# Gate and up: weight sums by adding transfers with turned signs, and the first block product by quarter blocks

## The chip, the cores and the metric

The kernel runs on one core of a Trainium2 chip. A core has five engines that work side by side, each through its own list of instructions in order: TensorE (PE) multiplies, VectorE (DVE) adds and subtracts, ScalarE (ACT) copies and applies functions, GpSimd (POOL) and SyncE (SP) mostly start transfers. Engines wait for each other by semaphores. The metric is the device time of one execution in microseconds (us).

## The reference, cut to what matters

One encoder layer on 1024 tokens of width 1024, all in float32. An input projection feeds eight heads of bidirectional retention and eight of windowed attention, an output projection and a layer norm give h, and then comes the part that is changed:

```python
g = jnp.einsum('bsd,df->bsf', h, w_ffn_gate[i].astype(jnp.float32))
up = jnp.einsum('bsd,df->bsf', h, w_ffn_up[i].astype(jnp.float32))
ffn = jnp.einsum('bsf,fd->bsd', jax.nn.silu(g) * up, w_ffn_down[i].astype(jnp.float32))
```

The hidden width is 2816, that is 22 tiles of 128. An embedding branch is added, and a second layer norm closes the layer.

## The kernel before, in words

**Precision.** A float32 operand is split into a high half (ACT copies it, rounded to fp32r, L1338) and a low half (DVE subtracts the high half from the operand, L1351). A product is three matmuls: high by high, high by low, low by high (`mm3c`, L874 to L876). So each prepared weight costs one ACT and one DVE instruction, and the third matmul of a group is the first that reads the low half.

**Pairs and block products.** The 22 hidden tiles are taken as pairs 0 to 10. For a pair, and for gate (m = 0) and up (m = 1), the weights are a 2 x 2 of blocks (i, j), i the hidden tile and j the half of the width; h is a 2 x 2 of width half and token half. The four blocks of the result come from seven block products instead of eight (Strassen and Winograd's scheme), numbered 1 to 7. They need sums of weight blocks (products 5, 6, 7, 3) and sums of blocks of h, made once. A *unit* is one product for one m: 12 matmuls of 512 columns into one PSUM bank. Products 1, 6, 7 and 4 go one after the other into the same two banks (the chain, named `bmm` in the profile); 5 and 3 share two others (`bt`). After product 1, ACT copies the running sum out (s1, L1510), after 6 (u2, L1512), after 7 (u3, L1517).

**Quarter blocks.** Product 2 from pair 1 on, and product 4 from pair 2 on, use the scheme once more: gate and up are the two rows, and seven products of 256 columns go in four parts of 18, 6, 6 and 12 matmuls (`FINE`, `prep_fine`, `mm_fine`, `post_fine`). Their parts stand between whole units, so that DVE can add the banks (`bo` for product 2, `bs` for product 4) into the results between parts.

**Weights and sums.** SP loads block rows of 512 KB: (0, j) into tiles called `raw`, (1, j) into tiles called `ln`. `sums` makes four sums per m on DVE (L1373, L1374, L1376, L1377); the quarter blocks make three of 256 columns and a difference (L1396 to L1398, L1413).

**Order.** `plan` writes the order of the units by hand. Preparation (`Piece`) runs ahead of the units: after each unit, `ahead_g` issues pieces until the time that it reckons for the next unit is used up, as long as one of eight operand tiles (`oslots`) is free; a piece of the next unit is always issued. Within ACT and DVE the pieces and the work after the units (`post`, `urgent`) so form one list each, and an instruction that waits holds up all behind it. At a pair's end `sums_down` makes four sums of results for the down projection (L1480), stored by SP. POOL has nothing to do in this stage.

Of the kernel before, what the change touches and what calls it, by code (L numbers as in the profile page):

```python
# [47 lines left out]
def layer(tc, xT, xn, w_first, w_mt, w_rv, w_out, w_pg, w_pe, pT, w_gu, w_dn,  # L48
# [1222 lines left out]
    FROM = {2: 1, 4: 2}  # L1271
# [3 lines left out]
    homes, sums2 = {}, []  # L1275
# [12 lines left out]
    def fine_right(p, places):  # L1288
# [15 lines left out]
        def make(q, left, right):  # L1304
            def steps(x, c, us):
                def rows(pair):
# [6 lines left out]
                        piece(0, us, parts=lambda: [(x, *(v[:, c, :] for v in place(q)))])]  # L1313

            if p == 2 or q in (7, 5):
                return steps(fwide, slice(0, 2), 0.68)
# [8 lines left out]
    class Piece:  # L1325
# [5 lines left out]
        def issue(self):  # L1331
# [3 lines left out]
            if self.parts:  # L1335
                held.extend((self, x) for x in self.parts())
                for _, (x, hi, lo) in held:
                    act.activation(hi, x, AF.Copy)  # L1338
# [7 lines left out]
    def release():  # L1346
        for _, x in held:
            if callable(x):
                x()
            else:  # L1350
                dve.tensor_tensor(x[2], x[0], x[1].bitcast(F32), ALU.subtract)  # L1351
        held.clear()

    class Pair:


        def __init__(self, n):
            self.n = n
            self.raw, self.ops, self.bank, self.ev, self.s, self.fb = {}, {}, {}, {}, {}, {}
            self.fine = {2: {}, 4: {}}  # L1360

        def load(self, m, part=(0, 1)):
            for i in part:
                r = rawt(2 * HF) if i == 0 else ct([P, D], "ln", 2)
                sp.dma_start(r, w_gu[2 * self.n + i, m])
                for j in range(2):
                    self.raw[m, i, j] = r[:, j * HF:(j + 1) * HF]

        def sums(self, p, m):
            a = lambda i, j: self.raw[m, i, j]  # L1370
            s = self.s.setdefault(m, [sums2[m][:, 0, :], sums2[m][:, 1, :], a(1, 0), sums2[m][:, 0, :]])
            if p == 6:
                dve.tensor_tensor(s[1], a(1, 0), a(1, 1), ALU.add)  # L1373
                dve.tensor_tensor(s[0], s[1], a(0, 0), ALU.subtract)  # L1374
            else:
                dve.tensor_tensor(a(1, 0), a(0, 0), a(1, 0), ALU.subtract)  # L1376
                dve.tensor_tensor(s[0], a(0, 1), s[0], ALU.subtract)  # L1377

        def prep(self, p, m):
            a = lambda i, j: self.raw[m, i, j]  # L1380
            s = self.s.get(m)
            src = {1: lambda: a(0, 0), 2: lambda: a(0, 1), 4: lambda: a(1, 1), 5: lambda: s[1], 6: lambda: s[0],
                   7: lambda: s[2], 3: lambda: s[3]}[p]()
            t = self.ops[p, m] = take_op()
            return [(src, t[:, 0, :], t[:, 1, :])]

        def prep_fine(self, p, part):
# [3 lines left out]
            def xy():  # L1391
                return [self.raw[m, p == 4, 1] for m in range(2)]
# [677 lines left out]
```

## Time and profile before

| What | us |
|---|---|
| median of 3 runs (lowest, highest) | 1167.75 (1167.6, 1168.26) |
| profiled execution, its own time | 1168.96 |
| its span, first to last instruction | 1167.2 |
| first and last load of gate and up weights, start | 522.4, 896.7 |

The profile page has one line per group: line, engine, operation, output and inputs, count, then busy time and mean duration in ns, then idle time before it and what ended it. A time line has the start in us, the duration, the instruction, and in brackets the idle time before it and its releaser. Matmuls overlap: their recorded durations (about 390 ns for 512 columns) are longer than the distance of their starts, and it is the distance that counts. `bmm`, `bt`, `bo`, `bs` are PSUM banks, `w` and `u` operand tiles, `ev` results.

### The profile page before, as it was taken

What the parts mean: (1) busy time and instruction counts of PE and PEld (TensorE: products, weight loads), DVE (VectorE), ACT (ScalarE), POOL (GpSimd) and SP (SyncE); (2) the same over time, 40 slices, a digit from 0 to 9 for tenths busy, and PEclk for the clock granted to TensorE, in tenths of its full rate; (3) what the DMA queues carried; (4) which work ended last, traced back from release to release, by engine and by line L of the source; (5) the groups of instructions that cost most, each with busy time, mean ns of one, the idle gap of its engine ahead of it and who ended that gap; (6) DMA issues with size and microseconds to landing.
All of it is one profiled execution on the core that took longest, in us unless ns stands there. A gap on an engine that the chain in (4) does not pass through costs nothing.

```text
span 1167.2 us, 19086 instructions
## 1 busy us (share of the span) xinstructions
PE 1151.9 (99%) x6978; PEld 965.8 (83%) x6978; DVE 895.7 (77%) x1687; ACT 564.4 (48%) x1162; POOL 105.1 (9%) x118
## 2 busy tenths in 40 slices
PE   9999999999999999999999999999999999999997
PEld 7888878777888888888888888888888888888886
DVE  5556678594858898948999988888888876774778
ACT  5645367666546366214444433443344445552462
POOL 2000010102010021000000000000000011124242
PEclk9999999999999999999999999999999999999999
DMA  6346777666567955756322332332223289999978
GB/s 251 103 159 214 258 241 232 211 210 194 154 216 241 365 178 185 269 193 210 112 96 98 115 107 98 103 134 101 100 73 136 83 249 344 348 236 217 256 172 233
DMA packets 88863, 218.64 MB, mean 187 GB/s; under 512 B 12544, under 2 KB 20928, under 8 KB 88768
## 3 DMA queue, kind: packets, MB, share of 16 engines
q1 hardware_dynamic: 79984, 200.11, 49.6%
q0 software_dynamic: 8784, 17.31, 8.4%
q8 instruction: 55, 0.90, 0.3%
q14 instruction: 40, 0.33, 0.1%
HBM read 143.35 MB, written 62.19 MB: 176 GB/s over the span
## 4 chain that ended last, share of the span: by engine, by line
PE 89%; issue 4%; DMA 3%; DVE 2%; ACT 1%; SPq 1%; POOL 0%; DVEq 0%; POOLq 0%; ACTq 0%
PE bmm L875 8%; PE bmm L874 8%; PE bmm L876 8%; PE bt L874 6%; PE bt L875 6%; PE bt L876 6%; PE bmm L82 4%; PE bmm L84 4%; PE bmm L83 4%; PE bs L876 4%; PE bs L875 4%; PE bs L874 4%; PE bo L876 4%; PE bo L875 4%; PE bo L874 4%
## 5 line engine op out<-in xcount | busy, mean ns | idle before, releaser
L82 PE MATMUL bmm<-H,w 128*128 128x512 f32 x240 | 97.2, 405 | 0.1
L84 PE MATMUL bmm<-H,w 128*128 128x512 f32 x240 | 94.0, 392 | 0.5 <-issue 0.5
L83 PE MATMUL bmm<-H,w 128*128 128x512 f32 x240 | 94.0, 392 | 0.0
L1474 ACT ACTIVATE ev<-ev 128x512 f32<-128x512 f32 x42 | 26.5, 630 | 105.0 <-DVE ev L1503 91.8
L1648 POOL DMA_DIRECT2D h0b<-in_w_dn x24 | 21.6, 900 | 537.7 <-DVE ev L1454 503.6
L82 PEld LDWEIGHTS bmm<-H,w 128*128 128x128 f32 x240 | 45.2, 188 | 12.2 <-issue 1.9
L84 PEld LDWEIGHTS bmm<-H,w 128*128 128x128 f32 x240 | 45.0, 188 | 10.2
L83 PEld LDWEIGHTS bmm<-H,w 128*128 128x128 f32 x240 | 45.1, 188 | 7.8
L582 ACT ACTIVATE sc<-sc,st 128x384 f32<-128x384 f32 (+1 forms) x64 | 37.3, 586 | 17.1 <-DVE st L579 17.0
L579 DVE CUSTOM_DVE_ANT_0 sc<-cst,bs,nskb 128x384 f32<-128x384 f32 (+1 forms) x64 | 35.2, 575 | 7.0 <-PE bs L578 6.9
L1503 DVE TENSOR_TENSOR ev<-ev,bt 128x512 f32<-128x512 f32 x44 | 30.0, 682 | 12.5 <-PE bt L876 12.5
L622 ACT ACTIVATE ptr<-bt 128x384 f32<-128x384 f32 (+1 forms) x64 | 26.5, 456 | 25.5 <-PE bt L617 25.4
L1454 DVE TENSOR_TENSOR ev<-ev,bs 128x256 f32<-128x256 f32 x63 | 25.5, 416 | 15.6 <-PE bs L876 14.7
L1476 DVE TENSOR_TENSOR ev<-ev 128x512 f32<-128x512 f32 x42 | 29.0, 691 | 10.5 <-ACT ev L1474 9.0
L77 DVE TENSOR_TENSOR w<-raw,w 128x512 fp32r<-128x512 f32 x34 | 23.0, 687 | 17.3 <-ACT w L76 16.7
L874 PE MATMUL bmm<-H,u 128*128 128x512 f32 x92 | 36.1, 392 | 0.0
L875 PE MATMUL bmm<-H,u 128*128 128x512 f32 x92 | 36.0, 392 | 0.0
L876 PE MATMUL bmm<-H,u 128*128 128x512 f32 x92 | 35.8, 389 | 0.0
L874 PE MATMUL bmm<-H,w 128*128 128x512 f32 x84 | 32.9, 392 | 0.0
L875 PE MATMUL bmm<-H,w 128*128 128x512 f32 x84 | 32.9, 392 | 0.0
L876 PE MATMUL bmm<-H,w 128*128 128x512 f32 x84 | 32.7, 389 | 0.0
L1454 DVE TENSOR_TENSOR ev<-ev,bo 128x256 f32<-128x256 f32 x70 | 28.3, 416 | 5.2 <-PE bo L876 4.5
(832 smaller groups left out, 3836.8 us busy)
## 6 DMA issues: line engine op xcount, KB each, us to landing
ad<-ev SPq DMA_DIRECT2D x33, 512.0 KB, 2.6
pgd<-pro SPq DMA_DIRECT2D x28, 512.0 KB, 3.3
raw<-in_w_gu SPq DMA_DIRECT2D x22, 512.0 KB, 4.0
ln<-in_w_gu SPq DMA_DIRECT2D x22, 512.0 KB, 4.6
raw<-ad SPq DMA_DIRECT2D x40, 256.0 KB, 6.2
ln<-ad SPq DMA_DIRECT2D x37, 256.0 KB, 6.3
H<-in_w_dn SPq DMA_DIRECT2D x33, 256.0 KB, 9.2
wod<-aq SPq DMA_DIRECT2D x16, 512.0 KB, 2.7
```

The source lines that it names most:

```text
L82: pe.matmul(o, lh, rh, start=start, stop=False)
L83: pe.matmul(o, lh, rl, start=False, stop=False)
L84: recent[0] = pe.matmul(o, ll, rh, start=False, stop=stop).ins.name
L579: dve.tensor_tensor_reduce(sc[g][:, :nk], cst[:, tc0:tc0 + nk], b[:, :nk], slope(i, g), nskb[:, 2 * i + g:2 * i + g + 1], ALU.add, ALU.min ...
L582: act.activation(sc[g][:, :nk], sc[g][:, :nk], AF.Exp, bias=st_[:, 0, j, g:g + 1], scale=-1.0, accum_out=st_[:, 2, j, g:g + 1])
L622: act.activation(p_[:, :hi - lo, :], tb[:, :hi - lo, :], AF.Copy)
L874: pe.matmul(o, lh, rh, start=start, stop=False, skip_group_check=True)
L875: pe.matmul(o, lh, rl, start=False, stop=False, skip_group_check=True)
L876: pe.matmul(o, ll, rh, start=False, stop=stop, skip_group_check=True)
L1454: dve.tensor_tensor(out_, x, b, ALU.add)
L1476: dve.tensor_tensor(c[:, 1, :], c[:, 0, :], c[:, 1, :], ALU.mult)
L1503: dve.tensor_tensor(get(name), ev[left][:, m, :], right, ALU.add)
```

## The change

**Signs.** The first block row is taken with turned sign: with A' = (-A00, -A01; A10, A11) all four sums of the scheme become sums of plain blocks: A10 + A11, then + A00, then + A01, and A00 + A10, the last two used with a minus. So each can grow in place: a transfer on POOL's queue with `accum_op=ALU.add` (`grow`) adds a block from memory onto the block that lies in SBUF, as soon as its last reader has prepared it (`after`). The DVE sums are gone; there are 88 such transfers of 256 KB. The minus sits in ACT's copy (`scale=-1.0`) and in DVE's low half (`scalar_tensor_tensor`).

**Product 1 by quarter blocks** from pair 4 on (`FROM[1] = 4`). Its result is s1 in SBUF (`post_first`), and `seed` copies it with ACT, negated, into the two chain banks, into which product 6 then accumulates. The fine difference is written into the (0, 0) block, so SP loads that block again before it grows.

**Order.** Product 5 moves ahead of 6, 7 follows, and product 1 of the next pair is woven into the end of a pair. From pair 4 on a pair reads: (5,0), 1 part 2, 2 part 0, 1 part 3, (5,1), 2 part 1, (6,0), 2 part 2, (6,1), 2 part 3, (7,0), (7,1), 4 part 0, (3,0), 4 part 1, (3,1), 4 part 2, next 1 part 0, 4 part 3, next 1 part 1, with parts numbered from 0. Operand tiles go from eight to seven. The core of the diff:

```diff
-    FROM = {2: 1, 4: 2}
+    FROM = {2: 1, 4: 2, 1: 4}
...
-                    act.activation(hi, x, AF.Copy)
+                for _, (x, hi, lo, *sign) in held:
+                    act.activation(hi, x, AF.Copy, scale=-1.0 if sign else 1.0)
...
+            elif len(x) == 4:
+                dve.scalar_tensor_tensor(x[2], x[0], -1.0, x[1].bitcast(F32), ALU.mult, ALU.subtract)
...
-        def sums(self, p, m):
-            a = lambda i, j: self.raw[m, i, j]
-            s = self.s.setdefault(m, [sums2[m][:, 0, :], sums2[m][:, 1, :], a(1, 0), sums2[m][:, 0, :]])
-            if p == 6:
-                dve.tensor_tensor(s[1], a(1, 0), a(1, 1), ALU.add)
-                dve.tensor_tensor(s[0], s[1], a(0, 0), ALU.subtract)
-            else:
-                dve.tensor_tensor(a(1, 0), a(0, 0), a(1, 0), ALU.subtract)
-                dve.tensor_tensor(s[0], a(0, 1), s[0], ALU.subtract)
...
+        def load(self, m, i, js=(0, 1)):
+            if (m, i) not in raws:
+                raws[m, i] = rawt(2 * HF) if i == 0 else ct([P, D], "ln", 2)
+            c = slice(js[0] * HF, (js[-1] + 1) * HF)
+            sp.dma_start(raws[m, i][:, c], w_gu[2 * self.n + i, m][:, c])
...
+        def grow(self, m, to, by):
+            pool.dma_start(self.block(m, *to), self.weights(m, *by), accum_op=ALU.add)
...
+        def after(self, p, m):
+            if p == 1:
+                if self.n >= FROM[1]:
+                    self.load(m, 0, (0,))
+                self.grow(m, (0, 0), (1, 0))
+            elif p == 5:
+                self.grow(m, (1, 0), (0, 0))
+            elif p == 6:
+                self.grow(m, (1, 0), (0, 1))
+            elif self.n + 1 < NP:
+                following = pairs2[self.n + 1]
+                if p == 7 and m:
+                    for k in range(2):
+                        following.load(k, 0)
+                elif p == 3:
+                    following.load(m, 1, (0,))
+                    following.grow(m, (1, 0), (1, 1))
+                elif p == 4:
+                    following.load(m, 1, (1,))
...
-            return [[piece(0, 1.16, main=sums), piece(1, 0.62, parts=whole), piece(1, 0.36, parts=lambda: put(5, fsum[0]))],
-                    [piece(1, 0.36, parts=lambda: put(6, fsum[1]))],
+                for m in range(2):
+                    self.after(p, m)
+
+            return [[piece(1, 0.62, parts=whole), piece(0, 1.16, main=sums), piece(1, 0.36, parts=lambda: put(5, fsum[0]))],
+                    [piece(1, 0.36, parts=lambda: put(6, fsum[1])), piece(0, 0.36, main=difference)],
                     [piece(0, 0.36, parts=lambda: put(7, fsum[2], 6))],
-                    [piece(1, 1.1, main=difference, parts=last, then=loads)]][part]
+                    [piece(1, 0.74, parts=last, then=loads)]][part]
...
+        def post_first(self, part):
+            if part == 0:
+                self.begin()
+                self.ev["s1"] = self.h["s1"]
+            (c11, c12), (c21, c22) = ([self.ev["s1"][:, m, j * Q:(j + 1) * Q] for j in range(2)] for m in range(2))
+            (ba, bb), bz = [self.fb[1][0][:, j * Q:(j + 1) * Q] for j in range(2)], self.fb[1][1][:, :Q]
+            if part == 0:
+                act.activation(c11, ba, AF.Copy)
+                dve.tensor_tensor(c11, c11, bb, ALU.add)
+            elif part == 1:
+                act.activation(c12, ba, AF.Copy)
+            elif part == 2:
+                act.activation(c22, ba, AF.Copy)
+                dve.tensor_tensor(c22, c22, bz, ALU.add)
+            else:
+                dve.tensor_tensor(c12, c12, bz, ALU.add)
+                act.activation(c21, ba, AF.Copy)
...
+        def seed(self):
+            for m in range(2):
+                self.bank[0, m] = bank(TAGS[0])
+                act.activation(self.bank[0, m], self.ev["s1"][:, m, :], AF.Copy, scale=-1.0)
...
+                if m and self.n >= FROM[1]:
+                    self.seed()
...
+    def plan():
+        two = lambda n, p: [(n, p, 0), (n, p, 1)]
+        fine = lambda n, p, *parts: [(n, p, None, j) for j in parts]
+        def start(n):
+            return fine(n, 1, 0) + fine(n, 1, 1) if n >= FROM[1] else two(n, 1)
+        u = start(0)
+        for n in range(NP):
+            a, b, c = two(n, 5), two(n, 6), two(n, 7) + (two(n, 4) if n < FROM[4] else [])
+            f = fine(n, 2, 0, 1, 2, 3)
+            if n < FROM[2]:
+                u += two(n, 2) + a + b
+            elif n < FROM[1]:
+                u += [f[0], a[0], f[1], a[1], f[2], b[0], f[3], b[1]]
+            else:
+                h = fine(n, 1, 2, 3)
+                u += [a[0], h[0], f[0], h[1], a[1], f[1], b[0], f[2], b[1], f[3]]
+            u += c
+            e, s = two(n, 3), start(n + 1) if n + 1 < NP else [None, None]
+            if n < FROM[4]:
+                u += e + s
+            else:
+                f = fine(n, 4, 0, 1, 2, 3)
+                u += [f[0], e[0], f[1], e[1], f[2], s[0], f[3], s[1]]
+        return [x for x in u if x]
...
```

**What stands where now.** Three places on which the prediction rests, all at the turn from pair 6 to pair 7; the turns from pair 3 to 4 up to 9 to 10 read alike. Names: `ev` results, `bs` the banks of product 4 (901 to 922) or product 2, `bo903` and `bo904` product 1's banks, `raw799` and `raw810` block row 0 of gate and of up, `ln811` and `ln812` block row 1, `cst` and `fs` quarter sums, `w` and `u` operand tiles. In brackets stand the semaphores waited for: `DMAHW` for SP's transfers, `DMASW` for POOL's, each in turn over eight numbers.

DVE, before, from the additions after product 4's last part (two L1454) on:

```order
L1454 TENSOR_TENSOR ev837_5573<-ev837_5573,bs922_7640 128x256
L1454 TENSOR_TENSOR ev837_5573<-ev842_5578,bs921_7639 128x256
L1476 TENSOR_TENSOR ev837_5573<-ev837_5573 128x512
L1480 TENSOR_TENSOR ev837_5573<-ev837_5573,ev841_5577 128x512
L1480 TENSOR_TENSOR ev841_5577<-ev837_5573,ev838_5574 128x512
L1480 TENSOR_TENSOR ev838_5574<-ev838_5574,ev837_5573 128x512
L1503 TENSOR_TENSOR ev840_5576<-ev840_5576,bt924_7692 128x512
```

DVE, changed, from the same additions (two L1478) on:

```order
L1478 TENSOR_TENSOR ev837_5575<-ev837_5575,bs902_7822 128x256
L1478 TENSOR_TENSOR ev837_5575<-ev842_5580,bs901_7821 128x256
L1529 TENSOR_TENSOR ev837_5575<-ev837_5575 128x512
L1533 TENSOR_TENSOR ev837_5575<-ev837_5575,ev841_5579 128x512
L1533 TENSOR_TENSOR ev841_5579<-ev837_5575,ev838_5576 128x512
L1533 TENSOR_TENSOR ev838_5576<-ev838_5576,ev837_5575 128x512
L1533 TENSOR_TENSOR ev840_5578<-ev840_5578,ev841_5579 128x512
L1417 TENSOR_TENSOR cst_367<-raw810_5485 128x256
L1418 TENSOR_TENSOR cst_367<-cst_367,raw799_5418 128x256
L1419 TENSOR_TENSOR fs834_5572<-raw799_5418,raw810_5485 128x256
L1355 TENSOR_TENSOR w821_5559<-raw799_5418,w821_5559 128x512
```

The fourth sum of results moved up, and the three quarter sums of the next product 2 and the low half of its first operand (`w821`) stand right behind the sums; behind them come one addition (L1501) and three low halves of 256, the last two for product 1's last part (`u826`). Before, the next product 2's quarter sums (L1396 to L1398) and the low half of its first operand stood five to thirteen instructions ahead of these additions, and three whole units lay between product 4's last part and product 2.

ACT, before, around the copies after product 6 (L1512) and after product 1 (L1510), with the bank to be read named after the arrow:

```order
L1510 ACTIVATE ev840_5576<-bmm938_8114 128x512 [waits PE_49]
L1338 ACTIVATE u822_5558<-ln931_7954 128x512 [waits DMAHW7_49,DVE_49,Activation_49]
L1338 ACTIVATE w823_5559<-raw930_7858 128x256 [waits Activation_49]
L1338 ACTIVATE w823_5559<-cst_367 128x256 [waits DVE_49]
L1512 ACTIVATE ev842_5578<-bmm937_8089 128x512 [waits DMAHW2_49,PE_49]
```

ACT, changed, around the new copies into the banks of product 6 (L1510, bank before the arrow):

```order
L1340 ACTIVATE u822_5560<-fs834_5572 128x256 [waits DVE_49]
L1340 ACTIVATE w825_5563<-ln812_5490 128x512 [waits DMASW5_49,Activation_49]
L1340 ACTIVATE w821_5559<-raw810_5485 128x256 [waits DVE_49,Activation_49]
L1340 ACTIVATE w821_5559<-raw799_5418 128x256 [waits DVE_49]
L1510 ACTIVATE bmm909_8055<-ev839_5577 128x512 [waits DVE_49]
L1510 ACTIVATE bmm910_8057<-ev839_5577 128x512 [waits Activation_49]
```

The copy of product 1 now writes the banks, and ahead of it stand three high halves; the first of them (`w825`, for the second unit of product 6) waits for a transfer of POOL's (`DMASW5`), the third in the list below.

POOL, changed (before, its list is empty here):

```order
L1380 DMA raw799_5418<-in_w_gu 128x512 [waits DMAHW1_49,DMAHW7_49,DMASW3_49,DVE_49]
L1380 DMA raw810_5485<-in_w_gu 128x512 [waits DMAHW2_49,DMAHW0_49,DMASW4_49]
L1380 DMA ln812_5490<-in_w_gu 128x512 [waits DMASW1_49,DVE_49]
L1380 DMA ln811_5487<-in_w_gu 128x512 [waits DMASW6_49,DMASW2_49,DVE_49]
L1380 DMA ln812_5490<-in_w_gu 128x512 [waits DMASW7_49,DMASW5_49,DVE_49]
```

The first two wait for SP's reloads of `raw799` and `raw810` (`DMAHW1`, `DMAHW2`), which in turn wait on SP for DVE's low halves of `u826`; the third, `ln812`, is queued behind them.

More of the change, by code (lines that the diff above doesn't have):

```diff
@@ L1274, in layer @@
     TAGS = {0: "t", 1: "o", 2: "mm", 4: "s"}
-    homes, sums2 = {}, []
+    homes, raws = {}, {}
+    AT = {1: (0, 0), 2: (0, 1), 4: (1, 1)}
+    made = set()
     def next_homes():
@@ L1312, in steps @@
                         piece(0, us, main=lambda: subtract(1)),
-                        piece(0, us, parts=lambda: [(x, *(v[:, c, :] for v in place(q)))])]
-            if p == 2 or q in (7, 5):
+                        piece(0, us, parts=lambda: [(x, *(v[:, c, :] for v in place(q)))], then=lambda: made.add((p, q)))]
+            if p == 2 or p == 4 and q in (7, 5):
                 return steps(fwide, slice(0, 2), 0.68)
@@ L1358, in __init__ @@
             self.n = n
[L1359 to L1367, printed above, removed]
-        def sums(self, p, m):
-            a = lambda i, j: self.raw[m, i, j]
-            s = self.s.setdefault(m, [sums2[m][:, 0, :], sums2[m][:, 1, :], a(1, 0), sums2[m][:, 0, :]])
-            if p == 6:
-                dve.tensor_tensor(s[1], a(1, 0), a(1, 1), ALU.add)
-                dve.tensor_tensor(s[0], s[1], a(0, 0), ALU.subtract)
-            else:
-                dve.tensor_tensor(a(1, 0), a(0, 0), a(1, 0), ALU.subtract)
-                dve.tensor_tensor(s[0], a(0, 1), s[0], ALU.subtract)
+            self.ops, self.bank, self.ev, self.fb = {}, {}, {}, {}
@@ L1391, in xy @@
             def xy():
-                return [self.raw[m, p == 4, 1] for m in range(2)]
+                return [self.block(m, *AT[p]) for m in range(2)]
             def sums():
@@ L1540, in g_unit @@
         pr = pairs2[n]
-        def loads():
-            if n + 1 < NP and p == 7 and m:
-                for j in range(2):
-                    pairs2[n + 1].load(j, (0,))
-        def more():
-            if n + 1 < NP and p == 4:
-                pairs2[n + 1].load(m, (1,))
-        items = [piece(1, 0.62, parts=lambda: pr.prep(p, m), then=more)]
-        if p in (6, 7):
-            items.insert(0, piece(0, 1.42 if p == 6 else 1.24, main=lambda: pr.sums(p, m), behind=loads))
-        after = {2: (0.62, 1.4), 5: (0.62, 1.4), 4: (0, 2.8), 3: (0.62, 2.1)}.get(p, (0, 0))[m]
+        items = [piece(1, 0.62, parts=lambda: pr.prep(p, m), then=lambda: pr.after(p, m))]
+        after = {2: (0.62, 1.4), 7: (0.62, 1.4), 4: (0, 2.8), 3: (0.62, 2.1)}.get(p, (0, 0))[m]
         return items, lambda: pr.mm(p, m), lambda: pr.post(p, m, k), 2.72, after
@@ L1943, in layer @@
         fine, more = fine_right(2, halves4[:3]), fine_right(4, halves4[3:])
-        fine += more
+        fine += more + fine_right(1, [(t[:, 0], t[:, 1]) for t in halves1])
         homes.update((name, a_tile([P, 2, HF], "ev")) for name in ("spare", "s1", "u2", "c11", "u3", "c22"))
-        FINE4 = len(plan(0)) + len(plan(1)) - 2
-        FINES = (2, 4, 7, 9, 20, 23, 26, FINE4)
+        fours = units.index((FROM[4] - 1, 4, 1))
+        FINES = (2, 4, 7, 9, 16, 19, 22, fours, fours + 3, fours + 8, fours + 13, units.index((FROM[1] - 1, 1, 1)))
         ahead_g(-1, 4)
```

91 lines of the change are left out of this document (47 added, 44 removed).

## The prediction

> **What bounds the kernel now.** I read the page's busy times first, then the gate-and-up stretch (about 530 to 930 us) by windows, then single instructions of that stretch in order of time.
>
> ```profile
> PE 1151.9 (99%) x6978; PEld 965.8 (83%) x6978; DVE 895.7 (77%) x1687; ACT 564.4 (48%) x1162; POOL 105.1 (9%) x118
> ```
> ```profile
> 600.00:700.00 100.00, 100.00 (x532) 86.40 (x531) 89.30 (x179) 41.84 (x85) 0.00 (x0) 1.00 0.28 99
> 700.00:800.00 100.00, 100.00 (x548) 87.09 (x547) 83.42 (x173) 42.61 (x87) 0.00 (x0) 1.00 0.29 99
> 800.00:900.00 100.00, 100.00 (x548) 87.09 (x547) 85.36 (x174) 44.02 (x90) 0.00 (x0) 1.00 0.35 119
> ```
>
> In the windows the columns are PE, PEld, DVE, ACT, POOL, then granted clock, DMA share and GB/s. PE has no gap. DVE is at 83 to 89 of 100 us, POOL is empty, DMA is below 0.35. So only two things change the time here: less PE work, or an operand that comes after PE wants it. DVE has 11 to 17 us of slack in 100, so its order decides whether an operand is late.
>
> **The change, part by part.** *PE, removed.* From pair 4 on, seven times, product 1 goes from two whole units to quarter blocks.
>
> ```profile
> 705.20 0.28 PE L874 MATMUL bo<-h0b,w 128*128 128x256 f32 x1
> ...
> 706.63 0.40 PE L874 MATMUL bmm<-H,w 128*128 128x512 f32 x1
> ...
> 709.38 0.28 PE L874 MATMUL bs<-h,u 128*128 128x256 f32 x1
> ...
> 711.53 0.40 PE L874 MATMUL bt<-H,w 128*128 128x512 f32 x1
> ```
> ```profile
> 762.82 0.39 PE L874 MATMUL bmm<-h0a,w 128*128 128x512 f32 x1
> ...
> 765.53 0.39 PE L874 MATMUL bmm<-h0a,u 128*128 128x512 f32 x1
> ...
> 768.25 0.28 PE L874 MATMUL bo<-h0b,w 128*128 128x256 f32 x1
> ```
>
> These are the first matmuls of units, so their distances are unit lengths. A whole unit (12 matmuls of 512) takes 2.71 us, two take 5.43. A quarter part of 18 matmuls takes 2.15, one of 12 takes 1.43, so one of 6 takes 0.72: together 2.15 + 2 x 0.72 + 1.43 = 5.02. Gain 0.41 a pair, 7 x 0.41 = **2.9 us**. That is all PE can give.
>
> *DVE, removed.* The four weight sums per product side go:
>
> ```profile
> L1374 DVE TENSOR_TENSOR sums<-sums,raw 128x512 f32<-128x512 f32 x22 | 15.2, 692 | 0.8
> L1373 DVE TENSOR_TENSOR sums<-ln 128x512 f32<-128x512 f32 x22 | 15.0, 684 | 0.0
> L1377 DVE TENSOR_TENSOR sums<-raw,sums 128x512 f32<-128x512 f32 x22 | 15.0, 683 | 0.0
> L1376 DVE TENSOR_TENSOR ln<-raw,ln 128x512 f32<-128x512 f32 x22 | 15.0, 683 | 0.0
> ```
>
> 60.2 us over eleven pairs, 5.5 a pair. Behind a full PE this is worth nothing by itself. It covers the right-hand quarter sums of product 1 (32 adds of 256 on DVE, 13 us at 0.42 each, made during pairs 0 to 3, where 22 us went); without that cover they would cost up to those 13 us. The sign (STT instead of TT) is free if it is priced like the row
>
> ```profile
> L959 DVE SCALAR_TENSOR_TENSOR acc<-acc,h0b 128x512 f32<-128x512 f32 x12 | 7.6, 684 | 0.0
> ```
>
> *First wait, DVE at the turn of a pair.* PE's new order after the last part of product 4 is: product 1 part 1 (0.72), first unit of product 5 (2.72), product 1 part 2 (0.72), then product 2 part 0.  Set t = 0 at the end of product 4's last part. PE reaches product 2 at 4.16, and its third matmul, which reads the low half, at 4.16 + 2 x 0.12 = 4.40. On DVE the order printed above puts ahead of that low half: two adds, the multiply after Silu, four sums, three quarter sums.
>
> ```profile
> 744.07 0.40 PE L874 MATMUL bmm<-H,u 128*128 128x512 f32 x1
> ```
> ```profile
> 744.27 0.75 DVE L1454 TENSOR_TENSOR ev<-ev,bo 128x256 f32<-128x256 f32 x2 [0.49 <-PE bo L876]
> ...
> 752.97 0.42 DVE L1396 TENSOR_TENSOR cst<-raw 128x256 f32<-128x256 f32 x1
> 753.42 0.42 DVE L1397 TENSOR_TENSOR cst<-cst,raw 128x256 f32<-128x256 f32 x1
> 753.76 0.42 DVE L1398 TENSOR_TENSOR fs<-raw,raw 128x256 f32<-128x256 f32 x1
> 754.10 0.68 DVE L1351 TENSOR_TENSOR u<-raw,u 128x512 fp32r<-128x512 f32 x1
> ...
> 762.24 0.69 DVE L1476 TENSOR_TENSOR ev<-ev 128x512 f32<-128x512 f32 x1 [1.08 <-ACT ev L1474]
> 762.97 2.02 DVE L1480 TENSOR_TENSOR ev<-ev,ev 128x512 f32<-128x512 f32 x3
> ```
> ```profile
> 744.72 0.63 ACT L1474 ACTIVATE ev<-ev 128x512 f32<-128x512 f32 x1 [0.77 <-DVE ev L1454]
> ```
>
> The adds start 0.20 after PE goes on (744.27 - 744.07). Silu starts 0.45 later and takes 0.63: 1.28. Multiply to first sum 0.73: 2.01. Three sums 2.02, the fourth 0.67: 4.70. Three quarter sums 1.13 (752.97 to 754.10): 5.83. Low half 0.68: **6.5**. PE waits 6.5 - 4.4 = **2.1 us**, every one of the seven times. Before, those quarter sums and that low half ran ahead of product 4's last additions, with three whole units (2.71 each) to spare.
>
> *Second wait, the transfers.* Behind that low half DVE does one add and three low halves of 256 (0.34 apart), so product 1's last operand is ready at 7.9. Only then may SP reload the (0,0) blocks, since the fine difference was written into them. POOL's queue then holds three adding transfers in this order: two onto the reloaded blocks, which must wait for the reloads, and behind them the one that product 6, second unit, needs.
>
> ```profile
> raw<-in_w_gu SPq DMA_DIRECT2D x22, 512.0 KB, 4.0
> ...
> ad<-ev SPq DMA_DIRECT2D x11, 256.0 KB, 2.0
> ...
> raw<-in_w_rv SPq DMA_DIRECT2D x8, 256.0 KB, 2.6
> ```
> ```profile
> L1648 POOL DMA_DIRECT2D h0b<-in_w_dn x24: 866/875/1194, 945.9 to 1120.6; - x24
> ...
> DMA to landing us min/median/max: 4.2/7.0/8.6
> ```
> ```profile
> q0 software_dynamic: 1440, 2.62, 24.6%
> ```
>
> The reload is 256 KB: between 2.6 (the 256 KB load) and 4.0 (the 512 KB one); I take 3.3, so it lands at 11.2, its twin 0.3 later. POOL issues take 0.88 each: 11.3, 12.2, third at 13.1. An adding transfer lands 4.2 to 7.0 after its issue, in the down stage, where SP's loads run beside it. Ten of them took 24.6% of 60 us of 16 engines (the last row, window 940 to 1000), 1.48 each, so the third may wait up to 2 x (1.48 - 0.88) = 1.2 for the two ahead. DMA is quiet here, so I take the minimum and half the queue: 13.1 + 4.2 + 0.6 = **17.9** (bounds 16.6, with the reload at 2.6 and no queue, and 20.8, with 4.0 and 7.0). [...]
>
> Who waits: ACT. Its next instruction is the high half of product 6's second unit, from that transfer. Behind it stand two copies of 256 and then the new copy of product 1 into the banks of product 6, and the *first* unit of product 6 cannot start without that copy.
>
> ```profile
> 777.61 0.62 ACT L1338 ACTIVATE w<-sums 128x512 fp32r<-128x512 f32 x1
> 778.14 0.41 ACT L1338 ACTIVATE u<-cst 128x256 fp32r<-128x256 f32 x1
> 778.44 0.62 ACT L1338 ACTIVATE w<-sums 128x512 fp32r<-128x512 f32 x1
> ```
>
> From landing to the copied bank: 0.53 + 0.30 + 0.30 + 0.62 = 1.75. PE starts product 6 at 19.7 (18.4 to 22.6). Without any wait it would be there at 4.16 + 2.15 + 1.43 + 2.72 + 0.72 = 11.2. Both waits together cost 19.7 - 11.2 = **8.5 us a turn** (7.2 to 11.4), 2.1 of it at product 2 and 6.4 in one piece at product 6. Nothing later gets it back: PE is the bound for the rest of the pair, and the next turn starts from PE's own end of product 4.
>
> *The clock after 6.4 us of idle.*
>
> ```profile
> 1.31 3.60 PE L147 MATMUL bo<-sq 128*128 128x512 bf16 x8 [1.31 <-POOL sq L144]
> 4.91 0.63 PE L82 MATMUL bmm<-H,w 128*128 128x512 f32 x1
> 5.37 0.39 PE L82 MATMUL bs<-H,w 128*128 128x512 f32 x1
> ```
> ```profile
> 236.45 0.44 PE L577 MATMUL bs<-k,aq 128*128 128x384 f32 x1 [1.68 <-DVE pt L446]
> ```
>
> At the kernel's start nine 512-column matmuls took 5.37 - 1.31 = 4.06 us, 0.45 each, twice the later 0.226 (2.71/12), although the clock column says 1.00. Such a restart loses 4.06 - 9 x 0.226 = 2.0 us. After the longest idle inside the kernel, 1.68 us, there is none. An idle of 6.4 is nearly four times that, nearer to a start than to a pause, so I take the 2.0 and keep 0 as the other end. [...]
>
> *At nothing.* 88 POOL issues (77 us) fall into an empty POOL. The new ACT work lies in ACT's slack (busy 42 to 44 of 100). In pairs 1 to 3 the same transfer follows product 5 without a reload: 7 us from issue, against three units and more until product 6's second half; at most 1 us in all.
>
> **The sum.** 7 x (8.5 + 2.0) - 2.9 = 70.6 us. The profiled execution of before took 1168.96 (span 1167.2), 1.2 above the median of 1167.75. From the median: **1238 us**.
>
> **Rivals.**
> (a) Both waits, no slow restart: 7 x 8.5 - 2.9 = 56.6, 1224 us. For it: the clock column reads 1.00 everywhere. Against it: the start. [...]
> (b) Transfers as slow as in the down stage (landing at 20.8): 7 x (11.4 + 2.0) - 2.9 = 91, 1259 us. For it: the median of 7.0. Against it: a DMA share of 0.3 here.
> (c) Only DVE is late, the transfers arrive in time: 7 x 2.1 - 2.9 = 11.8, 1180 us. It needs the third landing before about 11.6 (13.4, when PE gets there, less 1.75), 1.5 us before I have even its issue; only a much faster reload path would do it.
> (d) The other side, faster: 1167.75 - 2.9 = 1165. It decides if the three quarter sums and the low half of product 2 run on DVE ahead of the pair's last sums and the reload starts at t = 0 or earlier. The trace shows PE without any gap under a fuller DVE, which speaks for slack; the printed order of DVE and POOL speaks against it.
>
> **How the numbers follow.** Forecast 0.50, (a) 0.16, (b) 0.16, (c) 0.12, (d) 0.04, and 0.02 for a balance near zero. About 0.2% (2.3 us) is what a measurement of this kernel can tell from no change; (d) is just past it. Faster 0.04, same 0.02, slower 0.94. The forecast alone spans 7 x (7.2 + 0) - 2.9 = +47 to 7 x (11.4 + 2.0) - 2.9 = +91; I stretch this to 1195 and 1265, which leaves out (c), (d) and zero: 0.18.
>
> **What would show it.** In the changed profile: seven PE idles before product 6's first unit (first matmul of the bank chain), each about 6 us and released by ACT's copy; seven of about 2 us before product 2's third matmul, released by DVE's low half; ACT idle before a high half "from ln", released by a DMA; 512-column matmuls at 0.45 just after the long idles. In windows, PE below 85 in 100 from the fourth pair on and full before it. I am wrong if PE is full at the turn of pair 3 to 4, if the adding transfers land within 2 us, or if the idles stand elsewhere than at these two places.

## The result, and the profile after

The changed kernel takes 1252.86 us (median of 6 runs, 1251.13 to 1257.86) against 1167.78 for the kernel before in the same comparison (6 runs, 1167.54 to 1168.45): 1.0735 times as long, 95% interval 1.0715 to 1.0755, that is 85 us slower. Forecast were 1238, with 1195 to 1265 as the range. The profiled execution has a span of 1250.9 us, 83.7 more than before (1167.2).

The page's busy times first, then the waits of PE in the gate-and-up stretch (engine and line that waits, engine and line it waits for, then us in total, times, longest):

```profile
PE 1177.1 (94%) x7104; PEld 991.0 (79%) x7104; DVE 882.8 (71%) x1708; ACT 582.8 (47%) x1226; POOL 182.5 (15%) x206
```
```profile
PE bmm L874 <- ACT bmm L1510: 42.8, 7, 6.9
PE bs L876 <- DVE w L1355: 13.1, 7, 1.9
PE bs L874 <- DVE ev L1478: 3.4, 2, 3.1
PE bmm L874 <- ACT ev L1574: 2.0, 1, 2.0
```

PE had 99% and no gap; now it waits seven times for ACT's copy into product 6's banks (L1510) and seven times for DVE's low half (L1355), once each in every turn from pair 3 to 4 on. The last two rows are in no turn: two waits at pair 10's end (L1478), and one in pair 0 (L1574). These totals, and the brackets of the time lines, count idle time from the end that the profile gives the matmul before. From here on a wait is counted by distances of starts instead, beyond the distance of a full rate; that gives about 0.16 us more for each, 2.03 us where the bracket says 1.88.

By windows (columns as in the prediction):

```profile
540.00:690.00 150.00, 148.05 (x754) 126.22 (x753) 123.80 (x252) 67.89 (x135) 28.01 (x32) 1.00 0.66 157
690.00:740.00 50.00, 41.19 (x236) 36.32 (x236) 31.76 (x69) 18.93 (x42) 7.08 (x8) 0.93 0.56 137
740.00:790.00 50.00, 42.09 (x233) 37.27 (x232) 32.06 (x70) 18.94 (x42) 7.07 (x8) 0.90 0.53 132
```

Up to the fourth pair PE is full but for 2 us; then 8 to 9 of 50 us are lost, and the granted clock, 1.00 all through this stretch before, falls to 0.90 to 0.93. One turn in order of time, that from pair 4 to 5, with t = 0 at 739.86, the end of product 4's last part and the start of the next product 1's part 1. PE at t = 0, then DVE and SP:

```profile
739.86 0.28 PE L874 MATMUL bo<-u,u 128*128 128x256 f32 x1
```

```profile
741.91 2.62 DVE L1533 TENSOR_TENSOR ev<-ev,ev 128x512 f32<-128x512 f32 x4
744.45 0.42 DVE L1417 TENSOR_TENSOR cst<-raw 128x256 f32<-128x256 f32 x1
...
745.58 0.69 DVE L1355 TENSOR_TENSOR w<-raw,w 128x512 fp32r<-128x512 f32 x1
...
746.85 0.75 DVE L1355 TENSOR_TENSOR u<-raw,u 128x256 fp32r<-128x256 f32 x2
```
```profile
747.63 15.99 SPq L1373 DMA_DIRECT2D raw<-in_w_gu  x4
```

POOL, ACT and PE, with the third of POOL's transfers (issued at 753.01) in the view of DMA issues (KB each, us from issue to landing):

```profile
751.78 1.77 POOL L1380 DMA_DIRECT2D raw<-in_w_gu  x2 [15.60 <-DMA raw<-in_w_gu]
753.01 1.45 POOL L1380 DMA_DIRECT2D ln<-in_w_gu  x1
```
```profile
ln<-in_w_gu POOLq DMA_DIRECT2D x1, 256.0 KB, 6.0
```
```profile
759.14 0.63 ACT L1340 ACTIVATE u<-ln 128x512 fp32r<-128x512 f32 x1 [7.22 <-DMA ln<-in_w_gu]
...
760.28 1.10 ACT L1510 ACTIVATE bmm<-ev 128x512 f32<-128x512 f32 x2
```
```profile
746.32 0.39 PE L876 MATMUL bs<-h0b,w 128*128 128x256 f32 x1 [1.88 <-DVE w L1355]
...
747.13 0.34 PE L876 MATMUL bs<-H,u 128*128 128x256 f32 x1
747.27 0.42 PE L874 MATMUL bs<-H,u 128*128 128x256 f32 x1
747.48 0.42 PE L875 MATMUL bs<-H,u 128*128 128x256 f32 x1
...
750.47 0.36 PE L874 MATMUL bo<-h0a,u 128*128 128x256 f32 x1
750.66 0.28 PE L875 MATMUL bo<-h0a,u 128*128 128x256 f32 x1
750.78 0.28 PE L876 MATMUL bo<-h0a,u 128*128 128x256 f32 x1
```
```profile
760.92 0.80 PE L874 MATMUL bmm<-H,w 128*128 128x512 f32 x1 [6.04 <-ACT bmm L1510]
761.51 0.63 PE L875 MATMUL bmm<-H,w 128*128 128x512 f32 x1
761.94 0.63 PE L876 MATMUL bmm<-H,w 128*128 128x512 f32 x1
...
764.07 0.50 PE L875 MATMUL bmm<-H,w 128*128 128x512 f32 x1
764.41 0.39 PE L876 MATMUL bmm<-H,w 128*128 128x512 f32 x1
764.64 0.40 PE L874 MATMUL bmm<-H,w 128*128 128x512 f32 x1
```

The chain of the prediction is all there: sums, low half, PE; low halves, reload, POOL's three transfers, high half, copy, PE. The last two fences also show what to look for behind a wait: the distance of starts. Behind the long wait, matmuls of 512 columns start 0.43 apart instead of 0.23; behind the short one, those of 256 columns start 0.21 apart instead of 0.12, from 747.27 to 750.47. Such a stretch, in which matmuls start at nearly twice their usual distance, is called half rate below; the granted clock in these two is 0.50 (747.30 to 750.50, and 761.00 to 764.20).

Adding up every distance beyond the full-rate one between 495 and 1060 us gives the balance:

| Term | predicted, us | measured, us |
|---|---|---|
| seven waits at product 2 | 7 x 2.1 = 14.7 | 14.2 (2.03 each) |
| seven waits at product 6 | 7 x 6.4 = 44.8 | 43.9 (5.3 to 7.1, mean 6.27) |
| half rate behind the waits at product 6 | 7 x 2.0 = 14.0 | 13.5 |
| half rate behind the waits at product 2 | 0 | 7.9 (five of seven, 1.57 each) |
| pairs 1 to 3, the transfer behind product 5 | at most 1, not in the sum | 0 |
| pair 0, one wait | not named | 2.1 |
| pair 10's end, two waits and a half-rate stretch | not named | 5.3 |
| less TensorE work | -2.9 | -2.9 (not measured by itself) |
| sum | 70.6 | 84.0, span difference 83.7 |

### The profile page after: what moved, and what is told of

It reads as the page before. It is cut to its first block, busy times and chain, and to the rows that moved or that the text cites. A ratio compares the mean times of both kernels' runs of the same rounds, so it can differ in the third digit from the quotient of the medians.

```text
span 1250.9 us, 19801 instructions
## 1 busy us (share of the span) xinstructions
PE 1177.1 (94%) x7104; PEld 991.0 (79%) x7104; DVE 882.8 (71%) x1708; ACT 582.8 (47%) x1226; POOL 182.5 (15%) x206
## 4 chain that ended last, share of the span: by engine, by line
PE 77%; DMA 10%; DVE 7%; ACT 3%; issue 2%; POOL 1%; SPq 1%; DVEq 0%; ACTq 0%; POOLq 0%
PE bmm L874 7%; PE bmm L875 6%; PE bmm L876 6%; PE bs L876 5%; PE bs L874 5%; PE bs L875 5%; DMA ln<-in_w_gu 5%; PE bt L874 4%; PE bt L875 4%; PE bt L876 4%; PE bmm L82 4%; PE bmm L84 4%; PE bmm L83 4%; PE bo L876 2%; PE bo L874 2%; PE bo L875 2%
## 5 line engine op out<-in xcount | busy, mean ns | idle before, releaser
L1380 POOL DMA_DIRECT2D ln<-in_w_gu x66 | 60.7, 925 | 284.8 <-DMA ln<-in_w_gu 146.7
L82 PE MATMUL bmm<-H,w 128*128 128x512 f32 x240 | 97.4, 406 | 0.2
L84 PE MATMUL bmm<-H,w 128*128 128x512 f32 x240 | 94.2, 392 | 0.0
L83 PE MATMUL bmm<-H,w 128*128 128x512 f32 x240 | 94.1, 392 | 0.0
L1478 DVE TENSOR_TENSOR ev<-ev,bs 128x256 f32<-128x256 f32 x133 | 54.1, 418 | 30.7 <-PE bs L876 28.0
L874 PE MATMUL bmm<-H,w 128*128 128x512 f32 x100 | 41.7, 417 | 18.5 <-ACT bmm L1510 18.5
L874 PE MATMUL bmm<-H,u 128*128 128x512 f32 x76 | 34.0, 448 | 26.3 <-ACT bmm L1510 24.3
L1340 ACT ACTIVATE w<-ln 128x512 fp32r<-128x512 f32 (+1 forms) x56 | 33.0, 591 | 43.1 <-DMA ln<-in_w_gu 37.9
L1380 POOL DMA_DIRECT2D raw<-in_w_gu x22 | 21.0, 978 | 199.2 <-DVE w L1353 89.4
L1355 DVE TENSOR_TENSOR w<-ln,w 128x512 fp32r<-128x512 f32 (+1 forms) x40 | 25.0, 634 | 31.1 <-ACT w L1340 31.0
L1355 DVE TENSOR_TENSOR u<-ln,u 128x512 fp32r<-128x512 f32 (+1 forms) x35 | 21.0, 610 | 35.1 <-ACT u L1340 35.1
L1565 DVE TENSOR_TENSOR ev<-ev,bt 128x512 f32<-128x512 f32 x44 | 30.2, 686 | 19.2 <-ACT ev L1579 11.2
L875 PE MATMUL bmm<-H,w 128*128 128x512 f32 x100 | 40.7, 407 | 0.0
L874 PEld LDWEIGHTS bmm<-H,u 128*128 128x128 f32 x76 | 16.3, 214 | 30.6 <-ACT bmm L1510 25.1
L1340 ACT ACTIVATE u<-ln 128x512 fp32r<-128x512 f32 (+1 forms) x41 | 23.1, 569 | 37.2 <-DMA ln<-in_w_gu 31.5
L876 PE MATMUL bmm<-H,w 128*128 128x512 f32 x100 | 40.4, 404 | 0.0
```

The lines of the kernel that those rows point to most:

```text
L82: pe.matmul(o, lh, rh, start=start, stop=False)
L83: pe.matmul(o, lh, rl, start=False, stop=False)
L84: recent[0] = pe.matmul(o, ll, rh, start=False, stop=stop).ins.name
L874: pe.matmul(o, lh, rh, start=start, stop=False, skip_group_check=True)
L875: pe.matmul(o, lh, rl, start=False, stop=False, skip_group_check=True)
L876: pe.matmul(o, ll, rh, start=False, stop=stop, skip_group_check=True)
```

## Experiments

Times are medians against runs of the kernel before on the same chip, 1166.7 to 1168.0 us. t is counted in each trace from the end of product 4's last part at the turn of the same pair.

### Product 1 whole in every pair

```diff
-    FROM = {2: 1, 4: 2, 1: 4}
+    FROM = {2: 1, 4: 2, 1: 99}
```

> Product 1 stays whole in every pair; the adding transfers, the turned signs, the new order of the weight pieces and the operand tiles of the change all stay. My theory: both long waits of each turn (2.03 us at product 2, 6.27 at product 6) and the half-rate stretches behind them come from the weave of the quartered product 1 into product 4 and from what is queued behind it, none from the transfers as such; so both waits and the stretches go, the 2.1 us of pair 0 stays, and 1252.9 becomes 1168 to 1176. Rival (the adding transfers or their queue cost the time by themselves): near 1250.

(Product 1's quarter sums are also taken out of the lists of what is prepared; without the quarters, the units of a pair stand in the order of pairs 2 and 3.) 1176.61 us, ratio 1.0072 (1.0055 to 1.0088), 0.6 us past what the theory gave. All fourteen waits of the turns are gone. What is left of PE's waits:

```profile
PE bs L874 <- DVE ev L1478: 3.4, 2, 3.1
PE bmm L874 <- ACT ev L1574: 2.1, 1, 2.1
```

These are pair 10's end and pair 0, 6.0 us with what PE itself adds to each, and 4.3 us of half rate behind them; no TensorE work is saved here. So 76 of the 85 us come from the quartered product 1 with its reloads, as it is woven in, and the 88 adding transfers, which this kernel keeps, cost nothing in the turns. The two remaining waits belong to the other half of the change.

### Product 2's sums ahead of product 4's additions on DVE

```diff
-        while items and items[0].unit < upto and items[0].slots <= len(oslots) and (items[0].us <= room or items[0].unit <= k + 1):
+        far = 5 if k > 0 and units[k][1:] == (1, None, 0) else 1
+        while items and items[0].unit < upto and items[0].slots <= len(oslots) and (items[0].us <= room or items[0].unit <= k + far):
```

> VectorE makes the quarter sums and low halves of product 2's operand ahead of product 4's last additions; nothing else moves. My theory: the 2.03 us wait at product 2 goes, with the half-rate stretch behind it, but what the wait before product 6 hangs on (the reload, the three adding transfers, the copy) starts only as much earlier as VectorE comes to it earlier, and TensorE arrives 2 us earlier, so that wait keeps 6 to 8 us: only about 8 to 15 us are gained, 1238 to 1246. Rival (the two waits add, and each can be taken away alone): seven times 2.03 and the stretches of 1.57, 22 us or more, 1231 or less.

1262.58 us, ratio 1.0798 (1.0774 to 1.0822): 10 us slower than the change, where both theories had it faster. The edit moved half of what it should: the sums and the first low half went ahead, but the two low halves that release the reload stayed behind product 4's additions, whose stores now go out later. SP's last store and reload, in order of time, and the reload in the view of DMA issues (KB each, median us to landing), first of this kernel, then of the changed one:

```profile
746.50 0.45 SPq L1554 DMA_DIRECT2D ad<-ev  x1
747.84 17.82 SPq L1373 DMA_DIRECT2D raw<-in_w_gu  x3
```
```profile
raw<-in_w_gu SPq DMA_DIRECT2D x2, 256.0 KB, 5.7
```
```profile
744.56 0.45 SPq L1554 DMA_DIRECT2D ad<-ev  x1
```
```profile
raw<-in_w_gu SPq DMA_DIRECT2D x2, 256.0 KB, 3.5
```

With t = 0 at 740.42 the last store goes out at t = 6.1 instead of 4.7. The reload leaves 1.3 us behind the last of four stores (1.8 MB) instead of 3.1, and takes 5.7 us instead of 3.5. This turn is the one with the largest difference: over the turns the reloads whose landing is on record (10 of 14 in each trace) take 3.8 to 5.8 us, mean 4.8, instead of 2.6 to 3.8, mean 3.3. The wait at product 6 grows from 6.27 to 8.86 us (mean of seven): PE starts product 6 at a t that is 1.1 us later, and but for the wait would be there 1.5 us sooner. At product 2 a wait of 1.62 stays, now for a low half of 256 columns. Behind none of these seven is there half rate, which the 2.03 us waits had five times of seven.

### The adding transfers in another order

```diff
+                if m and self.n >= FROM[1]:          # behind the grow after product 5
+                    for k in range(2):
+                        self.after(1, k)
...
-                    self.after(p, m)
+                    if p != 1:
+                        self.after(p, m)
```

> The adding transfers that wait for the reload of raw are issued behind the one that is ready, so that the one for product 6's operand goes first. My theory: that transfer is issued some 4 to 7 us earlier, the copy into the banks follows, and the wait before product 6 falls from 6.3 us to about 2.3 or less, seven times 4: 1215 to 1225. The 2.03 us at product 2 stays. Rival (the adding transfer itself is the length of the wait, wherever it stands in its queue): unchanged, 1250 to 1255.

1227.59 us, ratio 1.0514 (1.0479 to 1.0548): 25 us of the 85 are gone, a little less than expected. The wait at product 6 falls to 3.19 us (mean of seven). POOL, and the landing of its first transfer:

```profile
745.81 0.88 POOL L1380 DMA_DIRECT2D ln<-in_w_gu  x1 [15.36 <-DVE raw L1437]
746.44 2.07 POOL L1380 DMA_DIRECT2D raw<-in_w_gu  x2
```
```profile
ln<-in_w_gu POOLq DMA_DIRECT2D x1, 256.0 KB, 4.2
```

Product 6's transfer goes first, at t = 11.7. That is hardly earlier than the first one went before (11.9), though nothing of it depends on the reload: it may go once DVE has made the low half of product 5's second operand (its releaser, L1437, stands right behind that), and both stand on DVE behind an addition that waits for product 2's first part, itself 2.03 us late. What it gains is its place in the queue. On the mean of the seven turns it is issued at t = 11.1, where it went third at 12.8, and it lands 4.2 us after its issue, where as the third it took 6.0. That is 3.5 us on its way, and the wait falls by 3.1 of its 6.3.

### The copy into the banks ahead of the transfer's high half

```diff
                 act.activation(c21, ba, AF.Copy)
+                self.seed()
...
-                if m and self.n >= FROM[1]:
-                    self.seed()
```

> ScalarE copies product 1's sums into product 6's banks ahead of the high half that waits for the third adding transfer; the transfers stay as they are. My theory: the first unit of product 6 no longer waits, the second one waits about 2 us for its operand, and fewer stretches run at half rate: 1205 to 1215. Rival (the operand, not the place of the copy, sets the wait): the wait only moves by one unit of 4 us, and the total stays above 1230.

1241.04 us, ratio 1.0623 (1.0607 to 1.0639). Product 6's first unit no longer waits, but the next part of product 2 does, 4.07 us on the mean. DVE and PE in the turn with the longest of these waits:

```profile
759.10 0.69 DVE L1355 TENSOR_TENSOR u<-ln,u 128x512 fp32r<-128x512 f32 x1 [6.43 <-ACT u L1340]
...
760.37 0.41 DVE L1478 TENSOR_TENSOR ev<-ev,bs 128x256 f32<-128x256 f32 x1
```
```profile
760.93 0.55 PE L874 MATMUL bs<-H,w 128*128 128x256 f32 x1 [5.89 <-DVE ev L1478]
```

The rival had it right. The addition that empties product 2's bank (L1478) stands on DVE behind the low half of the operand that comes with the late transfer. So the same transfer holds PE through ACT's queue or, if that way is cleared, through DVE's.

### Both together

> Both single edits at once: product 6's adding transfer is issued ahead of the two that wait for the reload, and ScalarE copies into the banks ahead of that transfer's high half. Each alone left a wait at product 6 (3.2 and 4.1 us on the mean), the first because the copy stands behind the transfer, the second because the transfer is late. My theory: together they leave next to nothing there (0 to 0.7 us a turn), the 2.03 us at product 2 stays with a half-rate stretch behind about half of them: 1190 to 1203. Rival (an adding transfer of 4 us cannot be hidden in this order at all): a wait of 2 to 3 us stays at product 6, 1212 to 1222.

1208.52 us, ratio 1.0351 (1.0336 to 1.0365), between the two theories. Waits of 0.3 to 1.3 us are left before that part of product 2, and a third one appears, 0.8 to 1.65 us before a later part of product 2. The 2.03 us waits stand unchanged, with half rate behind two of seven. Each edit alone was worth 25 and 12 us, both are worth 44.

### Another order of the units

```diff
-                u += [a[0], h[0], f[0], h[1], a[1], f[1], b[0], f[2], b[1], f[3]]
+                u += [a[0], h[0], h[1], a[1], f[0], f[1], b[0], f[2], b[1], f[3]]
```

(a, b: products 5 and 6; h: product 1's last parts; f: product 2.)

> As the run before, and in the order of the units product 1 part 3 and the second unit of product 5 go ahead of product 2 part 0, so that TensorE has 4.15 us more work before it needs product 2's low half. My theory: the 2.03 us wait goes too, no half-rate stretch is left in the turns, and what stays is pair 0's wait (2.1 to 2.4 us), pair 10's end (3.7) and a stretch of 1.6 to 2.8 behind each: 1171 to 1180. Rival (the reload and the growth of the first blocks, now last in the queue, are late for product 7 or for the next product 1): new waits there, 1190 or more.

1216.44 us (1.0422, 1.0390 to 1.0454). The time lies where the rival had it (1190 or more), but not for its reason, and the theory fell. The 2.03 us wait is gone. In its place come 0.98 us in each turn between product 1's parts 2 and 3, which now follow each other and use the same bank, and 3.5 us on the mean at product 2, again for an addition that DVE keeps behind a transfer's low half:

```profile
PE bs L874 <- DVE ev L1482: 23.4, 7, 3.9
PE bo L874 <- ACT ev L1504: 3.3, 7, 0.5
PE bo L874 <- DVE ev L1505: 1.3, 7, 0.2
```

All seven long waits are followed by half rate.

> As the run before, with pair 0's product 5 woven into product 2 and with the down stage's first splits issued later on VectorE, for the two waits outside the turns. My theory: all that the change lost is gone and the seven times 0.41 us of TensorE work remain as gain: 1165 to 1168. Rival (the splits, put off, are late for the down stage, or pair 0 keeps its wait): 1169 to 1176.

1218.13 us (1.0414, 1.0388 to 1.0439), outside both ranges: the waits of the turns are those of the run before (0.98 and 3.4 us, all seven with half rate). Weaving product 5 into product 2 in pair 0 took the wait there from 2.1 us (1.7 in the run before) to 0.3; putting off the down stage's splits did nothing for pair 10's end (0.42 and 3.29 us stay).

### How long an idle halves the rate

The kernel before, with idles made on purpose:

```diff
+        for _ in range((2, 3, 4, 5, 6, 8, 10)[rests[0] % 7]):
+            act.activation(idle, src, AF.Copy)
+        act.activation(idle, t[:, 1, :Q].bitcast(F32), AF.Copy)
+        act.activation(t[:, 0, :P], t[:, 0, :P].bitcast(F32), AF.Copy)
```

> The kernel before, with 24 pauses put in from pair 3 on: before the second unit of products 1, 6 and 5 ScalarE makes 2 to 10 copies of 256 columns from the bank of the work just ended and then writes a part of the unit's high half over itself, so that TensorE stands still for some 1.5 to 4 us. [...] Rival (the length of the pause decides by itself): one length divides all of them cleanly.

One run, 1332.72 us. ACT came later than reckoned, so the 24 idles are 2.5 to 9.1 us long and none is below 2.0. All are followed by half rate but the shortest:

```profile
786.49 0.50 PE L874 MATMUL bmm<-H,w 128*128 128x512 f32 x1 [2.35 <-ACT w L1570]
786.83 0.39 PE L875 MATMUL bmm<-H,w 128*128 128x512 f32 x1
787.05 0.39 PE L876 MATMUL bmm<-H,w 128*128 128x512 f32 x1
...
926.66 0.50 PE L874 MATMUL bt<-H,u 128*128 128x512 f32 x1 [2.58 <-ACT u L1570]
...
928.28 0.63 PE L874 MATMUL bt<-H,u 128*128 128x512 f32 x1
928.71 0.63 PE L875 MATMUL bt<-H,u 128*128 128x512 f32 x1
```

By itself this run fits the rival: one length between 2.51 and 2.74 us would divide them. Over all runs no length does: idles of 2.03 us were followed by half rate in 15 of 28 cases (five of seven in the changed kernel), while pair 0's idle of 2.1 us in the changed kernel, and idles of 2.99, 3.06, 3.17 and 3.31 us in the run with the other transfer order, were not. What divides them is not settled here.

### Mended versions

> From the last runs: product 1's parts 2 and 3 apart by a whole unit (next to each other they cost 0.98 us a turn), the low halves of product 5's second unit and of product 1's last part ahead of product 4's last additions, the copy into the banks ahead of, and the operand of product 6's second unit behind, the additions of product 2's first two parts on VectorE, so that no addition stands behind a transfer; the growth of the first blocks last in its queue; and in the last pair product 4's parts between whole units as before. My theory: no wait above 1 us is left in the turns nor at pair 10's end, and no half rate: 1165 to 1169, at best the 2.9 us of TensorE work. Rival (the adding transfers are late somewhere in any order of this kind): one wait of 1 us or more a turn, 1172 or more.

1242.14 us (1.0638, 1.0622 to 1.0653). The reload had slipped ahead of product 1's last operands, which then wait for it and read the reloaded blocks. So this kernel computes something else, and its time says only what a reload in the path costs. ACT shows it:

```profile
744.30 0.72 ACT L1340 ACTIVATE u<-raw 128x256 fp32r<-128x256 f32 x2 [8.85 <-DMA raw<-in_w_gu]
```

Its last pair, though, had product 4's parts between whole units again, and there 0.44 and 1.53 us were left of 0.42 and 3.27 and no half rate.

> The mended order once more, with two things put right. In the run before, the reload of the first blocks was issued ahead of product 1's last operands, which then read reloaded blocks: ScalarE waited 8.9 us for the reload, and the result was another one; here the reload and its growths follow product 1's last operands again, which in this order are prepared after product 5's second unit, so that product 6's adding transfer is still first in its queue. And product 2's parts 1 to 3 each move one unit on, so that none follows another directly (1.22 us a turn there), the last pair excepted. My theory: no wait above 1 us in the turns, no half rate, and 1.2 + 0.4 + 1.5 us of waits in the last pair against 2.9 us less TensorE work: 1166 to 1170. Rival (an adding transfer is late somewhere in any order of this kind): one wait of 1 us or more a turn, 1174 or more.

1174.40 us (1.0062, 1.0049 to 1.0074), above the theory's range. No wait of a turn is above 0.62 us, so the rival's long wait is not there either; 8.0 us of waits are left in all, and no half-rate stretch worth more than 0.4.

> The run before left 8 us of waits: seven or eight of 0.5 to 0.6 us before a part of product 4 or 2, whose bank VectorE empties only after quarter sums of a later product, and 1.2, 0.4 and 1.5 in the last pair. Here the planner reckons 2.6 us of VectorE work instead of 1.4 after product 7's second unit, so that the additions of product 4's first part come ahead of those sums, and the down stage's first splits come later. My theory: the 0.6 us waits of product 4 go (3.3 us in all), the last pair's 1.5 falls by about 0.5: 1169 to 1172, still not below the kernel before. Rival (the sums, put off, are late for the next product 1): a new wait of 0.5 us or more in each turn, 1174 or more.

This kernel's core differs from the changed kernel by

```diff
+                self.seed()                               # behind product 1's part 3
...
+                release()                                 # low halves ahead of product 4's last additions
...
-                u += [a[0], h[0], f[0], h[1], a[1], f[1], b[0], f[2], b[1], f[3]]
+                u += [a[0], h[0], a[1], h[1], f[0]]
+                u += [b[0], f[1], b[1], f[2], c[0], f[3], c[1]] if n < NP - 1 else [f[1], b[0], f[2], b[1], f[3]]
...
+        far = lambda x: x.unit <= k + 3 or units[x.unit][1:] != (6, 1) or units[x.unit][0] < FROM[1]
```

by 2.6 instead of 1.4 us reckoned after product 7, by pair 0 and the last pair ordered as in the runs above, and by the down stage's first splits put off. It took 1168.06 us against 1167.37: 1.0005, interval 0.9994 to 1.0016 (12 and 17 runs), no difference, and 0.9 us below the theory's range. Its waits of PE in the whole stretch, and one window of a turn:

```profile
PE bs L874 <- DVE ev L1478: 1.1, 1, 1.1
```
```profile
740.00:790.00 50.00, 50.00 (x296) 44.26 (x296) 40.50 (x90) 24.32 (x53) 8.15 (x10) 1.00 0.70 174
```

So the quartered product 1 with its reloads and all 88 adding transfers can run without a wait in the turns (the one left, 1.2 us, is in the last pair); it was the order, not the transfers, that cost the 85 us. The 2.9 us less of TensorE work do not show in the median. In the two profiled executions they are used up: from the same matmul ahead of this stage (number 3561, at 468.31 us before and 465.35 here) to its last one PE takes 690.93 us before and 690.79 here. Of the 2.9 us the wait left takes 1.2, and 1.6 go into small delays, a dozen of them of 0.05 to 0.2 us, five of these in pair 0. The span of 1165.1 us is 2.1 shorter than before, but not by the change: PE comes 3.0 us sooner to matmul 3561, and the work behind its last matmul takes 1.0 us longer. The twelve runs spread from 1164.4 to 1171.9.

## Why the prediction was right, step by step

- **First wait.** 2.1 forecast, 2.03 measured; the low half was done at t = 6.41 (745.58 + 0.69 - 739.86) where 6.5 was worked out. The step stands to a tenth.
- **Second wait, the chain.** Reload possible at 7.9: 7.77. Third transfer issued at 13.1: 13.15 in the turn shown (753.01 - 739.86), 12.8 on the mean of the seven. The reload was right (3.3 reckoned, 3.3 on the mean), and POOL's first two issues took 1.5 us on the mean instead of 1.8. Third transfer landed at 17.9: 19.2 in the turn shown, 18.8 on the mean. So the mis-sized term is the landing: 4.2 and 0.6 for the queue were reckoned, 4.8 us from issue, and 6.0 were measured (5.7 to 6.6). PE at product 6 at 19.7: 21.1 in the turn shown, 20.7 on the mean.
- **Why the wait still fitted.** 6.4 forecast, 6.27 measured on the mean, by two errors that cancel, which is luck: the copy came 1.0 us later, and PE came 1.1 us later, since in five of seven turns it ran at half rate behind the first wait. In the two turns without that half rate (first waits ending at 697.73 and 842.76) the second wait was 7.09 and 6.97, the two longest of the seven.
- **Slow clock.** 2.0 a turn behind the long waits: 1.9 on the mean, but 1.5 to 2.6 in single turns. The step that failed is the term left out behind the first wait. The prediction found no slow clock after an idle of 1.68 us and put none behind the 2.1 us waits either, without giving a reason. The brackets show 1.88 there, not far from 1.68, and half rate follows in five of seven turns, 1.57 us each, 7.9 us in all. It is the largest miss of the sum.
- **Left out.** Outside the turns the prediction weighed only the transfer behind product 5 in pairs 1 to 3, at most 1 us, and there nothing was lost. Pair 0 and pair 10's end are not in it, and cost 7.4: 2.1 and 5.3. At pair 10's end product 4's last two parts stand side by side, since no next product 1 follows, and DVE does the down stage's splits between them. I read the new order at the turns only.
- **Rivals.** (a), no slow restart, is out by the rows above. (b) gave 1259, the nearest number, but not for its reason: the third landing was at 18.8 on the mean, between the forecast's 17.9 and (b)'s 20.8, and the waits were 6.3, not 9.3. (c) and (d) ask for a faster or an earlier reload. The last mended kernel comes near (d) in one part: its reload goes out at t = 1.9 instead of 7.77. The other part of (d) it does not have: the three quarter sums still stand behind the pair's sums, and the first wait is gone because PE comes to product 2 only at t = 8.4 instead of 4.2. Without the waits it comes to no change rather than 1165.

What the experiments add to the chain of the prediction: it called the reload and the queue the cause of the second wait. They are, but clearing them one by one moved the wait to the next queue that holds something behind the transfer: the copy on ACT, then the addition on DVE, in two orders of the units.

## What to carry to other kernels

Where an instruction waits for a transfer, list what stands behind it on that engine; every short instruction there, such as an addition that only empties a bank, inherits the wait, and moving one of them only shows the next. Undo the whole order for one part (here product 1 whole) before mending single queues: that one run bounded the loss at 76 of 85 us, while six kernels with single queues or the order edited gave back between -10 and 44. And read the last repetition of a loop by itself: the part that normally fills a gap there is missing.

## What the runs showed of the hardware

**Half rate behind idles.** In the kernel before, PE has no gap between 495 and 1060 us and the granted clock is 1.00 throughout. In the changed kernel it is 0.50 in 13 stretches between 709.67 and 1033.94 us, eight of 3.41 us and five of 6.83, and 1.00 between them (as from 744.00 to 747.00 and from 764.80 to 767.00). By the idle just ahead, counted by distances of starts:

| PE's idle in the changed kernel | us | times | granted clock behind it |
|---|---|---|---|
| pair 0 | 2.1 | 1 | 1.00 |
| before product 2 | 2.03 | 7 | 0.50 five times, 1.00 twice (behind 697.73 and 842.76) |
| before product 6 | 5.3 to 7.1 | 7 | 0.50 every time |
| pair 10's end, first wait | 0.42 | 1 | 1.00 |
| pair 10's end, second wait | 3.29 | 1 | 0.50 |

In the other runs, by the distances of starts: none of the seven waits of 1.62 us was followed by half rate in the kernel with product 2's sums ahead on DVE; four idles of 2.99, 3.06, 3.17 and 3.31 us were not in the run with the other transfer order; in the run with made idles the one of 2.51 us was not, and all from 2.74 us on were. So a wait cost more than its own length, in the changed kernel 1.57 us more behind five of the seven of 2.03 us and 1.9 us more on the mean behind those of 5.3 to 7.1. Which waits of 2 to 3.3 us are followed by half rate, and why, is not settled here.

**A load behind stores.** At the turn shown the reload of 256 KB took 3.5 us when issued 3.1 us behind the last of 1.8 MB of stores, and 5.7 us when issued 1.3 us behind it; over the turns the means are 3.3 and 4.8. That the distance to the stores is the cause is not shown: in the last mended kernel reloads issued 34 us behind the last store took 4.1 to 4.6.

**Adding transfers one behind the other.** In the changed kernel three adding transfers of 256 KB are issued within 1.2 to 1.7 us in each turn. On the mean of the seven turns the first lands 4.0 us after its issue, the second 5.3 and the third 6.0.
